# The up-projection of a gated MLP by seven block products in place of eight

## The chip, the cores and the metric

The kernel runs on one core of a Trainium2 chip. The metric is the device time of one execution in microseconds (us). Below, PE is the matrix engine, DVE the vector engine, ACT the scalar engine, POOL the GpSimd engine and SP the engine that only issues DMAs here.

## The reference, cut to what matters

One layer of a hybrid backbone on 128 context tokens and 512 latent tokens: a token mixer (retention beside attention, merged, projected) and then the MLP that the change is about. Both groups of tokens use the same weights and only the modulation differs, so the kernel treats them as 640 columns.

```python
def conv_ffn(h, w_up, conv_w, conv_b, w_down):      # h (L, 1024), w_up (1024, 5632), w_down (2816, 1024)
    L = h.shape[1]
    u = h @ w_up
    up = jnp.pad(u, ((0, 0), (1, 1), (0, 0)))
    uc = conv_w[0] * up[:, :L] + conv_w[1] * up[:, 1:L + 1] + conv_w[2] * up[:, 2:L + 2] + conv_b
    a, g = jnp.split(uc, 2, axis=-1)
    return (jax.nn.silu(g) * a) @ w_down
...
        h = rmsnorm(xs, norm2_g[l]) * (1.0 + sc2) + sh2
        xs = xs + g2 * conv_ffn(h, w_up[l], conv_w[l], conv_b[l], w_down[l])
```

The result then passes a last RMSNorm with `final_g`.

## The kernel before, in words

All matrices are fp32. A product of two fp32 matrices is made of three PE products of rounded parts: each operand is split into a high part (a cast) and a low part (the operand minus its high part), and high·high, high·low and low·high are summed in PSUM. A weight block of 128 x 1024 is loaded as `raw` (2 buffers), cast by ACT into a `wh` tile (L143) and its low part subtracted by DVE into another `wh` tile (L148); there are 8 `wh` tiles. In the variant "dma", ACT writes the negated high part (L145) and a DMA issued from POOL adds `raw` to it (L146).

The region of the change is the second half of the program. First comes the output projection with the second normalisation: `h2_norm` (L1031 to L1034) scales a block of 128 tokens, `h2_trans` (L1043 to L1055) transposes it on PE and writes the high and low parts of the activations, h, as `hT` (128 x 8 x 640 each). Then the MLP: its 2816 channels are 22 blocks f of 128. For each f and each half i (i = 0 the part `a`, i = 1 the gate `g`), `up_cols` makes u = w_up·h by two PSUM tiles of 320 columns of tokens, of 24 matmuls each (8 blocks of the depth times 3, L1107 to L1109); ACT copies them into a `u` tile (L1113, L1114) that has zero columns between and around the two sequences. `up_gate` is the convolution of three taps (ACT L1121, DVE L1122 and L1123), then gating (ACT tanh L1127, DVE L1128 and L1129) and the split of the gated tile `gt` into high (ACT L1130) and low (POOL L1131). For f = 0 and 1 `up_cols` runs first on 256 columns, between the last transposes, and then on 384.

The down-projection takes a group of f (2, then 4 at a time): ten PSUM tiles of 512 columns with 12 matmuls per group of four, each then multiplied by a gate row and added to the residual by DVE (L1168, L1169). Up- and down-projection alternate: the up-projection of the next four f, then the down-projection of the four before. In the last group `square` (L1174) and `finish` (L1178 to L1188) make the last RMSNorm. `gate_rows` (L270) makes the gate rows between the first f and the loop, on PE.

The order of PE's instructions is the order of the code in the stretches under `manual_schedule`; elsewhere a scheduler sets each engine's queue when the program is built. Every engine takes its queue in order. PSUM has eight tiles of 512 columns: before, 3 for the up-projection (`mm`) and 5 for the down-projection (`acc`).

## Time and profile before

| what | value |
|---|---|
| median of three runs | 1215.33 us (1214.75 to 1215.36) |
| the profiled execution's own time | 1216.4 us |
| its span in the trace | 1214.6 us |
| PE busy | 1181.1 us, 97% of the span |
| DVE busy | 679.3 us, 56% |
| ACT busy | 488.0 us, 40% |
| POOL busy | 138.3 us, 11% |

The span is the time from the first to the last instruction that the trace shows; the execution's own time has another 1.8 us around it. A timeline row has a start, a duration, an engine, a line, the operation, what it writes and reads, its shape, and in brackets the idle time of its engine just before it with what ended it. Matmuls overlap, so the time that one takes of PE is read from the distance of two starts and not from its duration.

### The profile page before, as it was taken

Reading aid. Unit: us, or ns where it says so; the run is one execution under the profiler, and the core shown is the slowest. Engines: PE = TensorE matmul, PEld = TensorE weight load, DVE = VectorE, ACT = ScalarE, POOL = GpSimd, SP = SyncE. Lnnn points to the kernel's source line nnn. Section 1 sums busy time; section 2 is a strip of 40 time slices with the busy share of each in tenths; the row PEclk is TensorE's granted clock in tenths of the full one; section 3 lists DMA queues with packets and bytes.
Section 4 is the critical chain, followed back from the end, with each engine's and each line's share of the span. In section 5 each row is a group of like instructions: output and inputs, shape, how many; then the busy total and the mean of one; then the engine's idle time right before and its main releaser. Section 6 shows DMA issues by size and latency. Waiting matters only on the chain.

```text
span 1214.6 us, 18211 instructions
## 1 busy us (share of the span) xinstructions
PE 1181.1 (97%) x7545; PEld 1071.4 (88%) x7545; DVE 679.3 (56%) x1211; ACT 488.0 (40%) x881; POOL 138.3 (11%) x142
## 2 busy tenths in 40 slices
PE   4999999999999999999999999999999999999995
PEld 3788899999988888789999889999989989989984
...
GB/s 284 260 117 70 36 35 36 36 70 206 170 191 140 150 85 73 6 70 68 72 70 70 156 71 158 70 63 111 70 72 67 70 105 55 85 71 97 76 1 87
DMA packets 106387, 115.42 MB, mean 95 GB/s; under 512 B 25136, under 2 KB 77440, under 8 KB 106304
## 3 DMA queue, kind: packets, MB, share of 16 engines
...
## 4 chain that ended last, share of the span: by engine, by line
PE 93%; DVE 3%; ACT 1%; issue 1%; POOL 1%; DMA 0%; SPq 0%; DVEq 0%; ACTq 0%; POOLq 0%
DMA xin.u1.1_112<-in_x_sample 0%; POOL f0.s.5_3525 L898 0%; ACT gt.gt0.2_6393 L1051 0%; DVE x1.u1.1_6381 L1027 0%; PE mm1.mm.11_318 L155 0%; DVE acts.u2.2_101 L1055 0%; PE mm1.mm.11_318 L157 0%; POOL f0.s.5_3525 L921 0%; PE mm3.mm.40_4503 L155 0%; PE mm3.mm.36_4220 L155 0%; PE mm3.mm.22_3753 L155 0%; PE mm3.mm.40_4503 L157 0%; PE mm3.mm.37_4500 L155 0%; PE mm1.mm.12_319 L155 0%; PE mm3.mm.37_4500 L157 0%
## 5 line engine op out<-in xcount | busy, mean ns | idle before, releaser
L787 POOL TENSOR_TENSOR ret.r2k.6_3635<-ret.u5.5_3528,ret.u1.1_3521 128x256 f32<-128x256 f32 x2 | 1.4, 737 | 204.3 <-ACT ret.u5.5_3528 L783 204.3
L1184 POOL TENSOR_TENSOR x1.u1.1_6381<-x1.u1.1_6381,t7.u6.6_6913 128x512 f32<-128x512 f32 x5 | 6.4, 1285 | 43.4 <-ACT x1.tm.95_10737 L1174 23.5
L836 DVE SCALAR_TENSOR_TENSOR ret2.u1.1_4322<-ret2.u1.1_4322,const.u14.14_94 64x128 f32<-64x128 f32 x24 | 6.8, 338 | 6.4 <-ACT ret2.u1.1_4322 L829 6.3
L352 PE MATMUL mm1.mm.1_180<-const.u1.1_70,xin.u1.1_112 128*128 128x128 f32 x4 | 1.1, 435 | 9.3 <-DVE xin.u1.1_112 L345 9.3
L838 DVE SCALAR_TENSOR_TENSOR ret2.u1.1_4322<-ret2.u1.1_4322,const.u14.14_94 64x128 f32<-64x128 f32 x24 | 6.6, 379 | 4.7 <-ACT ret2.u1.1_4322 L831 4.7
L148 DVE TENSOR_TENSOR weights.wh.183_6567<-weights.raw.181_6564,weights.wh.182_6566 128x1024 fp32r<-128x1024 f32 x1 | 1.2, 1226 | 14.2 <-ACT weights.wh.182_6566 L143 14.2
L352 PEld LDWEIGHTS mm1.mm.1_180<-const.u1.1_70,xin.u1.1_112 128*128 128x128 f32 x4 | 0.7, 218 | 9.5 <-DVE xin.u1.1_112 L345 9.5
L389 ACT CAST acts.u1.1_100<-f0.s.1_113 128x640 fp32r<-128x640 f32 x4 | 2.9, 729 | 14.3 <-DVE f0.s.1_113 L387 14.3
L789 DVE TENSOR_TENSOR ret.u5.5_3528<-ret.u5.5_3528,ret.u1.1_3521 128x512 f32<-128x512 f32 x5 | 3.5, 692 | 9.2 <-POOL ret.r2k.8_3706 L787 3.2
L789 DVE TENSOR_TENSOR ret.u4.4_3527<-ret.u4.4_3527,ret.u1.1_3521 128x512 f32<-128x512 f32 x5 | 3.5, 692 | 8.9 <-POOL ret.r2k.11_3886 L787 4.7
L521 POOL TENSOR_TENSOR p1.u1.1_618<-p1.u3.3_622,p1q.u1.1_612 128x512 f32<-128x512 f32 x1 | 1.3, 1297 | 60.8 <-DMA p1.vc.6_627<-in_cache_v 60.8
L898 POOL TENSOR_TENSOR f0.s.5_3525<-f0.s.5_3525,ret2.ny20.11_4904 128x512 f32<-128x512 f32 x5 | 6.0, 1237 | 9.1 <-DVE ret2.ny20.11_4904 L215 9.1
L490 ACT ACTIVATE f0.s.3_724<-f0.s.3_724,p1q.ny20.11_892 128x128 f32<-128x128 f32 x20 | 6.0, 389 | 2.5 <-DVE p1q.ny20.11_892 L213 2.5
L148 DVE TENSOR_TENSOR weights.wh.108_4352<-weights.raw.106_4349,weights.wh.107_4351 128x1024 fp32r<-128x1024 f32 x1 | 1.2, 1226 | 10.1 <-ACT weights.wh.107_4351 L143 10.1
L389 ACT CAST acts.u1.1_100<-f0.s.2_114 128x640 fp32r<-128x640 f32 x4 | 2.9, 728 | 9.8 <-DVE f0.s.2_114 L387 9.8
L1055 DVE TENSOR_TENSOR acts.u2.2_101<-gt.gt0.2_6393,acts.u1.1_100 128x512 fp32r<-128x512 f32 x10 | 6.8, 686 | 0.0
L1131 POOL TENSOR_TENSOR gt.gt1.14_9296<-t7.tg.51_9431,gt.gt0.13_9295 128x641 fp32r<-128x641 f32 x1 | 2.0, 1952 | 39.3 <-PE mm7.mm.58_9464 L1108 39.3
L1131 POOL TENSOR_TENSOR gt.gt1.12_8594<-t7.tg.39_8729,gt.gt0.11_8593 128x641 fp32r<-128x641 f32 x1 | 1.9, 1936 | 39.2 <-PE mm7.mm.42_8762 L1108 39.2
L143 ACT CAST weights.wh.112_4507<-weights.raw.111_4505 128x1024 fp32r<-128x1024 f32 x1 | 1.0, 1047 | 13.0 <-PE mm3.mm.36_4220 L156 13.0
L255 DVE COPY mod2.wr.9_4312<-aux3.aux.15_4279 128x128 f32<-128x128 f32 x1 | 0.3, 292 | 10.7 <-PE aux3.aux.15_4279 L252 10.7
L336 ACT ACTIVATE acts.u2.2_101<-xin.u1.1_112 128x1024 fp32r<-128x1024 f32 x5 | 5.3, 1056 | 2.5 <-DMA xin.u1.1_112<-in_x_prompt 1.7
L490 ACT ACTIVATE f0.s.4_973<-f0.s.4_973,p1q.ny20.20_1141 128x128 f32<-128x128 f32 x20 | 6.2, 399 | 0.0
...
## 6 DMA issues: line engine op xcount, KB each, us to landing
xin.u1.1_112<-in_x_sample SPq DMA_DIRECT2D x4, 512.0 KB
...
```

What stands on the lines that cost most here:

```text
L148: (lo_eng or V).tensor_sub(lo, rv, hi.bitcast(F32))
L336: nc.scalar.activation(sq, xin[:, t, :], AF.Square, accum_out=ss[:, t:t + 1])
L352: nc.tensor.transpose(ps[:, j * P:(j + 1) * P], xin[:, t, k * P:(k + 1) * P], ident)
L389: nc.scalar.copy(hT[0][:, k, :], xk)
L490: nc.scalar.activation(x[:, j], x[:, j], AF.Copy, scale=rstd[:, j:j + 1])
L789: V.tensor_mul(z, z, r1[:, t, 0:1, :].to_broadcast([P, 8, 64]))
L836: V.scalar_tensor_tensor(Ss[0:64, hh, st + 1, j], Ss[0:64, hh, st, j], cdsel[0:64, h:h + 1], Ss[0:64, hh, st + 1, j], op0=ALU.mult, op1=AL ...
L838: V.scalar_tensor_tensor(Ss[64:128, hh, 2 - st, j], Ss[64:128, hh, 3 - st, j], cdsel[64:128, h:h + 1], Ss[64:128, hh, 2 - st, j], op0=ALU. ...
L898: nc.gpsimd.tensor_mul(ov, ov, rso[:, 4 * t:4 * t + 4].unsqueeze(2).to_broadcast([P, 4, P]))
L1055: V.tensor_sub(d[1], h3, d[0].bitcast(F32))
L1131: nc.gpsimd.tensor_sub(gt[1][:, fi, :641], tg, gt[0][:, fi, :641].bitcast(F32))
L1184: nc.gpsimd.tensor_mul(x1[:, t, lo], x1[:, t, lo], fg[:, lo])
```

## The change

The 2816 channels are 11 pairs of f. For 9 of the 11 pairs (f = 4 to 21), and for each half i of these, the product of 256 output channels, a depth of 1024 and the tokens is made by Strassen's method: channels, depth and tokens are each halved, and seven products of sums of blocks replace the eight products of blocks. Such a product of a pair and a half is called a unit below; there are 18.

- To halve the tokens evenly, h is stored with the zero columns that the convolution wants: two halves of 322 columns (`HW`), so `h2` is 128 x 8 x 644 and a PSUM tile has 322 columns.
- Four sums of activation blocks are made once (`diff`, `neg_sum`, `hi_of`, `lo_of`, L1168 to L1184): DVE instructions on 128 x 1288 elements, eleven ahead of the loop and three more later, with their high parts on ACT.
- `unit_group` makes a unit. Its products come in the order 1, 5, 6, 2, 7, 3, 4, each 12 matmuls of 322 columns. The weight blocks are summed in place by four DVE additions (128 x 4 x 128, L1285) per unit. A product's weights are one `wh` tile with a high half (ACT L1288) and a low half: by DVE (L1293) for five products, and for products 2 and 3 by ACT (L1290) and an accumulating DMA from POOL (L1291).
- Products share PSUM tiles: 1, 6, 7 and 4 accumulate one after another in one tile, 5 and 3 in a second, 2 has a third. Between them partial sums are copied out: ACT copies after 1 (L1312), 6 (negated, L1316), 7 (L1320) and 4 (L1324) and after 5 (negated, L1314), and DVE adds or subtracts after 2 (L1318), 7 (L1321) and 3 (L1330). Product 6 therefore starts only when ACT has copied the tile after 1, 7 when it has copied after 6, and 4 when it has copied after 7. One other product lies between each two of them on PE.
- PSUM is four `mm` and four `acc` tiles. The `wh` tiles are filled ahead of their use as the 8 buffers allow (`pump`): eight products ahead in the units.
- The down-projection's weights are split with "dma" in all groups but the last. The gated tiles hold two f in place of four; gating writes into the tiles of the convolution.
- In the last group f = 18 and 19 come first for the first four token blocks, in eight PSUM tiles, then f = 20 and 21 are added to each. The columns of the projection ahead of the MLP are made one token block earlier (`out_half`), and the low parts of the first weights are placed elsewhere there.

```diff
+        def prod(m):
+            def go():
+                q = {1: 1, 6: 1, 7: 1, 4: 1, 2: 2, 5: 3, 3: 3}[m]
+                if m in (1, 2, 5):
+                    st[q] = mm([P, 512], tag="mm")[:, :HW]
+                ps, (ah, al), (bh, bl) = st[q], AOP[m], ops[m]
+                for k in range(4):
+                    nc.tensor.matmul(ps, bh[:, k], ah[:, k], start=m in (1, 2, 5) and k == 0, stop=False,
+                                     skip_group_check=m in (3, 4, 6, 7))
...
+                if m == 1:
+                    nc.scalar.copy(u[0][:, lo_u], ps)
+                elif m == 5:
+                    nc.scalar.activation(u[1][:, hi_u], ps, AF.Copy, scale=-1.0)
+                elif m == 6:
+                    nc.scalar.activation(u[1][:, lo_u], ps, AF.Copy, scale=-1.0)
+                elif m == 2:
+                    V.tensor_add(u[0][:, lo_u], u[0][:, lo_u], ps)
+                elif m == 7:
+                    nc.scalar.copy(u3[i], ps)
+                    V.tensor_sub(u[1][:, hi_u], u[1][:, hi_u], u3[i])
+                    V.memset(u[1][:, 642:643], 0)
+                elif m == 4:
+                    nc.scalar.copy(u[0][:, hi_u], ps)
...
+                else:
+                    V.tensor_sub(u[1][:, lo_u], u[1][:, lo_u], ps)
...
+                if add:
+                    V.tensor_add(src, src, bs[add])
+                t_ = wp([P, 1024], F32R, tag="wh", bufs=8)
+                hi, lo = (t_[:, z * 512:(z + 1) * 512].rearrange("p (k n) -> p k n", n=P) for z in range(2))
+                nc.scalar.copy(hi, src)
+                if m in (2, 3):
+                    nc.scalar.activation(lo, src, AF.Copy, scale=-1.0)
+                    nc.gpsimd.dma_start(lo, src, accum_op=ALU.add)
+                else:
+                    V.tensor_sub(lo, src, hi.bitcast(F32))
...
+    groups = [plain_group(1, 0)] + down_groups([0, 1]) + [plain_group(1, 1)]
+    for p in range(2, NF // 2):
+        groups.append(unit_group(p, 0))
+        if p % 2:
+            groups += down_groups(list(range(2 * p - 4, 2 * p)))
+        groups.append(unit_group(p, 1))
...
+        for t in range(NT - 1):
+            for c0, n in cols[t]:
+                last_mm(t, c0, n, (0, 1))
+        for t in range(NT):
+            for c0, n in cols[t]:
+                last_mm(t, c0, n, (2, 3) if t < NT - 1 else (0, 1, 2, 3))
+                down_add(bank[t, c0], t, c0)
```

ACT's queue in the middle of the loop, before: two f of the up-projection. `weights.wh` are the weight tiles, `mm7` the PSUM tiles, `cv` the convolution's tiles, `tg` the tanh, `gt` the gated tiles.

```order
L1127 ACTIVATE t7.tg.39_8729<-t7.cv.38_8725 128x641
L1113 COPY t7.u3.3_6898<-mm7.mm.41_8735 128x128
L1114 COPY t7.u3.3_6898<-mm7.mm.41_8735 128x192
L143 CAST weights.wh.264_8857<-weights.raw.263_8855 128x1024
L1130 CAST gt.gt0.11_8593<-t7.tg.39_8729 128x641
L143 CAST weights.wh.266_8861<-weights.raw.263_8855 128x1024
L1114 COPY t7.u3.3_6898<-mm7.mm.42_8762 128x320
```

The same queue in the changed kernel, one unit (its tile for products 1, 6, 7 and 4 is mm.37, that for 5 and 3 mm.38, that for 2 mm.39):

```order
L1312 COPY t7.u1.1_6919<-mm7.mm.37_9190 128x322
L1314 ACTIVATE t7.u3.3_6921<-mm7.mm.38_9212 128x322
L1288 CAST weights.wh.310_9205<-weights.raw.300_9046 128x512
L1141 CAST gt.gt0.17_9155<-t7.cv.36_8825 128x641
L1316 ACTIVATE t7.u3.3_6921<-mm7.mm.37_9190 128x322
L1138 ACTIVATE t7.tg.41_9230<-t7.cv.40_9208 128x641
L1288 CAST weights.wh.311_9227<-weights.raw.300_9046 128x512
L1288 CAST weights.wh.312_9249<-weights.raw.300_9046 128x512
L1290 ACTIVATE weights.wh.312_9249<-weights.raw.300_9046 128x512
L1288 CAST weights.wh.313_9268<-weights.raw.300_9046 128x512
L1320 COPY const.u1.1_70<-mm7.mm.37_9190 128x322
```

A PSUM tile's copy had two or three instructions on weights and gating ahead of it in the queue; each of the copies L1316 and L1320 now has between one and five ahead of it since the copy before, and a product of PE waits for each.

DVE's queue in the middle of the loop, before:

```order
L1128 SCALAR_TENSOR_TENSOR t7.tg.51_9431<-t7.tg.51_9431,t7.cv.50_9427 128x641
L1129 TENSOR_TENSOR t7.tg.51_9431<-t7.tg.51_9431,t7.cv.49_9423 128x641
L148 TENSOR_TENSOR weights.wh.295_9560<-weights.raw.293_9557,weights.wh.294_9559 128x1024
L148 TENSOR_TENSOR weights.wh.297_9564<-weights.raw.293_9557,weights.wh.296_9563 128x1024
L1122 SCALAR_TENSOR_TENSOR t7.cv.52_9543<-t7.u3.3_6898,t7.u5.5_6912,t7.cv.52_9543 128x641
```

And in the changed kernel, beside the ACT rows above (same unit):

```order
L1129 SCALAR_TENSOR_TENSOR t7.cv.40_9208<-t7.u2.2_6920,t7.u5.5_6927,t7.cv.40_9208 128x641
L1139 SCALAR_TENSOR_TENSOR t7.cv.38_9163<-t7.tg.39_9184,t7.cv.38_9163 128x641
L1285 TENSOR_TENSOR weights.raw.300_9046<-weights.raw.300_9046 128x4x128
L1140 TENSOR_TENSOR t7.cv.36_8825<-t7.cv.36_8825,t7.cv.38_9163 128x641
L1293 TENSOR_TENSOR weights.wh.310_9205<-weights.raw.300_9046,weights.wh.310_9205 128x512
L1130 SCALAR_TENSOR_TENSOR t7.cv.40_9208<-t7.u2.2_6920,t7.u5.5_6927,t7.cv.40_9208 128x641
L1285 TENSOR_TENSOR weights.raw.300_9046<-weights.raw.300_9046 128x4x128 x2
L1139 SCALAR_TENSOR_TENSOR t7.cv.40_9208<-t7.tg.41_9230,t7.cv.40_9208 128x641
L1293 TENSOR_TENSOR weights.wh.311_9227<-weights.raw.300_9046,weights.wh.311_9227 128x512
L1140 TENSOR_TENSOR t7.cv.37_8855<-t7.cv.37_8855,t7.cv.40_9208 128x641
L1318 TENSOR_TENSOR t7.u1.1_6919<-t7.u1.1_6919,mm7.mm.39_9253 128x322
```

ACT's casts L1288 now wait for DVE's sums L1285, and its cast L1141 for DVE's product L1140; on DVE these stand between the convolutions and the low parts.

DVE's queue at the start of the loop, in the changed kernel. The 1288 elements are sums of activation blocks; `weights.wh.204` is the low part of the second half of the weights of the first plain group, f = 2 and 3:

```order
L1170 TENSOR_TENSOR gt.gt0.5_7252<-gt.gt0.5_7252,acts.u2.2_101 128x1288
L1130 SCALAR_TENSOR_TENSOR t7.cv.8_7212<-t7.u3.3_6921,t7.u5.5_6927,t7.cv.8_7212 128x641
L1129 SCALAR_TENSOR_TENSOR t7.cv.9_7216<-t7.u4.4_6922,t7.u5.5_6927,t7.cv.9_7216 128x641
L1184 TENSOR_TENSOR sums.u4.4_6913<-gt.gt1.6_7253,sums.u3.3_6912 128x1288
L1130 SCALAR_TENSOR_TENSOR t7.cv.9_7216<-t7.u4.4_6922,t7.u5.5_6927,t7.cv.9_7216 128x641
L1184 TENSOR_TENSOR sums.u6.6_6915<-gt.gt0.5_7252,sums.u5.5_6914 128x1288
L1139 SCALAR_TENSOR_TENSOR t7.cv.7_7208<-t7.tg.10_7270,t7.cv.7_7208 128x641
L151 TENSOR_TENSOR weights.wh.204_7293<-weights.raw.199_7284,weights.wh.203_7292 128x1024
```

Before, only the convolutions and the gating of f = 0 and 1 stood there; the low part of those weights now comes behind the eleven sums.

## Rows read from the trace of the kernel before

**Rows 1.** The page's busy time of the engines, with the share of the span and the count of instructions, and the engines' shares of the chain that ended last.

```profile
PE 1181.1 (97%) x7545; PEld 1071.4 (88%) x7545; DVE 679.3 (56%) x1211; ACT 488.0 (40%) x881; POOL 138.3 (11%) x142
...
PE 93%; DVE 3%; ACT 1%; issue 1%; POOL 1%; DMA 0%; SPq 0%; DVEq 0%; ACTq 0%; POOLq 0%
```

**Rows 2.** PE's waits: what waited for what, the sum in us, the count, the longest. The longest of all, and the only one behind 650 us.

```profile
PE mm1.mm.1_180 L352 <- DVE xin.u1.1_112 L345: 9.3, 1, 9.3
...
PE aux3.aux.99_7036 L1043 <- DVE gt.gt0.1_6392 L1034: 1.1, 1, 1.1
```

**Rows 3.** Busy time by stretch: the stretch and its length, busy time of PE, PEld, DVE, ACT and POOL with counts, the granted clock of PE, the DMA share, GB/s. The loop, and the out-projection ahead of the MLP.

```profile
766.00:1180.00 414.00, 414.00 (x2492) 388.57 (x2491) 251.36 (x286) 163.26 (x266) 36.01 (x23) 1.00 0.23 74
...
700.00:746.00 46.00, 44.87 (x264) 39.41 (x263) 36.82 (x115) 22.65 (x51) 7.50 (x18) 1.00 0.62 94
```

**Rows 4.** PE's timeline in the loop: the first matmuls of two tiles of the up-projection that follow each other, of 24 matmuls each.

```profile
850.52 0.31 PE L1107 MATMUL mm7.mm.25_8033<-acts.u1.1_100,weights.wh.224_7895 128*128 128x320 f32 x1
...
854.04 0.31 PE L1107 MATMUL mm7.mm.26_8060<-acts.u1.1_100,weights.wh.224_7895 128*128 128x320 f32 x1
```

**Rows 5.** ACT's timeline in the loop: a PSUM copy, the first tap of a convolution, tanh, the cast of a gated tile, the cast of a weight block.

```profile
850.72 0.43 ACT L1114 COPY t7.u2.2_6897<-mm7.mm.24_7993 128x320 f32<-128x320 f32 x1 [3.03 <-PE mm7.mm.24_7993 L1109]
851.18 0.93 ACT L1121 ACTIVATE t7.cv.26_8023<-t7.u2.2_6897,t7.u5.5_6912 128x641 f32<-128x641 f32 x1
854.05 0.74 ACT L1127 ACTIVATE t7.tg.27_8027<-t7.cv.26_8023 128x641 f32<-128x641 f32 x1 [1.94 <-DVE t7.cv.26_8023 L1123]
...
856.81 0.73 ACT L1130 CAST gt.gt0.9_7891<-t7.tg.27_8027 128x641 fp32r<-128x641 f32 x1
857.61 1.05 ACT L143 CAST weights.wh.236_8159<-weights.raw.233_8153 128x1024 fp32r<-128x1024 f32 x1
```

**Rows 6.** DVE's timeline in the loop: a tap, a step of the gating, two low parts of weights; and POOL's low part of a gated tile, which ran beside the second of them.

```profile
852.14 0.89 DVE L1122 SCALAR_TENSOR_TENSOR t7.cv.26_8023<-t7.u2.2_6897,t7.u5.5_6912,t7.cv.26_8023 128x641 f32<-128x641 f32 x1 [5.23 <-ACT t7.cv.26_8023 L1121]
...
854.82 0.83 DVE L1128 SCALAR_TENSOR_TENSOR t7.tg.27_8027<-t7.tg.27_8027,t7.cv.26_8023 128x641 f32<-128x641 f32 x1 [0.87 <-ACT t7.tg.27_8027 L1127]
...
856.93 1.23 DVE L148 TENSOR_TENSOR weights.wh.235_8156<-weights.raw.233_8153,weights.wh.234_8155 128x1024 fp32r<-128x1024 f32 x1 [0.42 <-ACT weights.wh.234_8155 L143]
858.70 2.00 DVE L148 TENSOR_TENSOR weights.wh.237_8160<-weights.raw.233_8153,weights.wh.236_8159 128x1024 fp32r<-128x1024 f32 x1 [0.54 <-ACT weights.wh.236_8159 L143]
...
857.66 1.96 POOL L1131 TENSOR_TENSOR gt.gt1.10_7892<-t7.tg.27_8027,gt.gt0.9_7891 128x641 fp32r<-128x641 f32 x1 [24.56 <-PE mm7.mm.26_8060 L1108]
```

**Rows 7.** The timelines of four engines ahead of the loop: PE's last matmul on tile mm.96; ACT's instructions up to its copy of that tile and one copy of 512 columns; a tap on DVE that lay beside POOL's low part of a gated tile.

```profile
762.38 0.34 PE L1109 MATMUL mm3.mm.96_7163<-acts.u1.1_100,weights.wh.196_6927 128*128 128x384 f32 x1
...
761.89 1.05 ACT L145 ACTIVATE weights.wh.204_7270<-weights.raw.202_7267 128x1024 fp32r<-128x1024 f32 x1
762.85 1.03 ACT L143 CAST weights.wh.205_7274<-weights.raw.202_7267 128x1024 fp32r<-128x1024 f32 x1
763.79 0.47 ACT L1114 COPY t7.u4.4_6899<-mm3.mm.96_7163 128x384 f32<-128x384 f32 x1
764.16 0.58 ACT L272 COPY gate.u1.1_5311<-mm7.mm.1_7228 128x512 f32<-128x512 f32 x1
...
761.18 2.23 DVE L1123 SCALAR_TENSOR_TENSOR t7.cv.10_7206<-t7.u3.3_6898,t7.u5.5_6912,t7.cv.10_7206 128x641 f32<-128x641 f32 x1
...
761.13 1.59 POOL L1131 TENSOR_TENSOR gt.gt1.6_7191<-t7.tg.9_7200,gt.gt0.5_7190 128x641 fp32r<-128x641 f32 x1 [21.47 <-ACT gt.gt0.5_7190 L1130]
```

**Rows 8.** The last group's timelines: PE's first matmuls of two tiles of the down-projection, of 12 matmuls each and 512 columns; DVE's evacuation of a tile; the first `finish` on DVE, its end and what comes behind it; the last evacuation, of 256 columns.

```profile
1181.75 0.39 PE L155 MATMUL acc7.acc.54_10775<-weights.wh.349_10711,gt.gt0.15_9997 128*128 128x512 f32 x1
...
1184.54 0.39 PE L155 MATMUL acc7.acc.55_10793<-weights.wh.344_10701,gt.gt0.15_9997 128*128 128x512 f32 x1
...
1187.60 0.69 DVE L1168 TENSOR_TENSOR x1.tm.102_10806<-acc7.acc.55_10793,gate.u1.1_5311 128x512 f32<-128x512 f32 x1 [1.38 <-PE acc7.acc.55_10793 L157]
1188.33 0.69 DVE L1169 TENSOR_TENSOR x1.u1.1_6381<-x1.u1.1_6381,x1.tm.102_10806 128x512 f32<-128x512 f32 x1
...
1194.52 0.16 DVE L1178 TENSOR_REDUCE t7.ss3.73_10847<-x1.u3.3_6383 128x3 f32<-128x9 f32 x1
...
1200.20 0.68 DVE L1168 TENSOR_TENSOR x1.tm.108_10894<-acc7.acc.58_10881,gate.u1.1_5311 128x512 f32<-128x512 f32 x1
...
1203.79 0.43 DVE L1168 TENSOR_TENSOR x1.tm.114_10948<-acc7.acc.61_10935,gate.u1.1_5311 128x256 f32<-128x256 f32 x1
```

**Rows 9.** Timelines at the start of the MLP: the last scaling of a token block on DVE; PE's first matmul on 384 columns, and its first of the gate rows behind 96 such; DVE's last low part of the activations.

```profile
741.14 0.75 DVE L1034 TENSOR_SCALAR gt.gt0.1_6392<-x1.u1.1_6381,x1.ny1.42_6877 128x1024 f32<-128x1024 f32 x1
...
745.75 0.34 PE L1107 MATMUL mm3.mm.93_7085<-acts.u1.1_100,gt.gt1.3_6586 128*128 128x384 f32 x1
...
762.56 0.61 PE L270 MATMUL mm7.mm.1_7228<-const.u1.1_70,const.u6.6_86 128*128 128x128 f32 x4
...
745.96 0.69 DVE L1055 TENSOR_TENSOR acts.u2.2_101<-gt.gt0.2_6393,acts.u1.1_100 128x512 fp32r<-128x512 f32 x1
```

**Rows 10.** The chain of waits: one of the four stretches of gate rows on PE (start, length, tile, line).

```profile
762.72 0.89 PE mm7.mm.1_7228 L270 x8
```

**Rows 11.** DMA issues: an accumulating DMA from POOL, its size and the us from issue to landing.

```profile
weights.wh.204_7270<-weights.raw.202_7267 POOLq DMA_DIRECT2D x1, 512.0 KB, 4.5
```

334 lines of the change are left out of this document (224 added, 110 removed).

## The prediction, made before the changed kernel ran

> **What bounds the kernel now.** I read the page's busy shares first, then PE's waits, then busy time by stretch, and last the timelines of the loop, since the change lies there. PE is busy for 97% of the span and is 93% of the chain that ended last [rows 1]; its longest wait behind the first microseconds is 1.1 us, ahead of the MLP [rows 2]. In the loop from 766 to 1180 us PE is busy for 414.00 of 414 us at a granted clock of 1.00, while DVE is busy for 251 (61%) and ACT for 163 (39%) [rows 3]. So every microsecond of matmul taken from the loop comes off the time, as long as DVE and ACT deliver weights and copies in time. The reader is to see that PE never waits in the loop, that DVE has some 160 us of idle time there, and that each tile of the up-projection costs the other engines one copy only.
>
> **Matmuls removed.** Two tiles' starts lie 854.04 − 850.52 = 3.52 us apart for 24 matmuls of 320 columns, 0.1467 us each [rows 4]. A tile of the down-projection takes 2.79 us for 12 of 512, 0.2325 each [rows 8]: per column 0.458 and 0.454 ns, so columns set the price, and 322 cost 0.1476. A unit had 4 tiles of 24, 14.08 us, and has 84 matmuls, 12.40 us. That is 1.68 us less, and for 18 units **−30.2 us**. The two pairs that stay get 4 more columns in each of 8 x 24 matmuls: 192 x 4 x 0.458 ns = **+0.35**.
>
> **Handovers in a unit.** This is the wait that the change adds. A product lasts 12 x 0.1476 = 1.77 us. Product 6 may start when ACT has copied the shared tile after 1, and product 5 lies between; so ACT has 1.77 us from one product's end to the next one's start. A copy of 320 columns takes 0.43 us and begins 0.2 us after the next tile's first matmul (850.72 against 850.52 [rows 4, 5]): ACT may come 1.1 us late at no cost. What stands ahead of the copy in ACT's queue decides. Casts of half a tile: 0.58 us by the copy of 512 columns [rows 7]; a tap 0.93, tanh 0.74, the cast of a gated tile 0.73 [rows 5]. Rows 7 show such a lateness: the copy of mm.96 began at 763.79, though its last matmul had started at 762.38 and lasted 0.34, because two weight instructions of 1 us stood ahead. One instruction of that kind fits into the slack and two do not.
>
> Worse is an instruction ahead of the copy that itself waits for DVE: ACT's cast of a block sum waits for DVE's addition, and the cast of the gated tile for DVE's product. DVE's load in four units: 36 additions and low parts of 512 at 0.69 [rows 8] = 24.8; 12 evacuations of 322 columns, between 0.43 for 256 and 0.69 for 512 [rows 8], 0.50 = 6.0; 16 taps at 0.89 and 8 gating steps at 0.83 [rows 6] = 20.9. That is 51.7 us in 49.6 us of PE. Queued independent instructions start a little closer than their durations (1188.33 − 1187.60 = 0.73 is a dependent pair), so 48 to 52. Behind four units come two groups of the down-projection, 10 tiles x 2.79 = 27.9 us, with 20 x 0.69 = 13.8 us of DVE: over the period of 77.5 us DVE has 65.5, 85%. ACT has in four units 36 x 0.58 + 20 x 0.43 + 8 x 0.93 + 4 x 1.47 = 42.8 us, 86%. Weights are made eight products, 14 us, ahead, so PE will not starve for weights; the copies, in the same queues, have no such lead.
>
> I followed both queues by hand through a period in the order in which they stand, with these durations, each instruction starting when its engine was free and its inputs were there. With the durations whole, the four units lost 0.3, 0.4, 1.2 and 1.7 us = 3.6; with successive instructions overlapping by a tenth, 0, 0, 0.95 and 0.95 = 1.9. The late ones are those in which gating and the sums of the next unit meet. For 4.5 periods: 8.6 to 16 us. The bounds lie further apart: nothing, if the queues interleave better than I followed, and 38 (rival C). I take **+14**, near the upper figure, since DVE is at 97% to 105% of PE's time in the units.
>
> **The start.** DVE is busy for 36.8 of 46 us in the out-projection [rows 3], and the scaling that releases the last transposes at 741.14 [rows 9] ended PE's 1.1 us [rows 2]. Two low parts of 1.23 us [rows 6] now stand in that stretch: +2.4 (0 to 4). Then the first plain group wants its second weights 17.0 us (4 tiles of 388 columns, from 16.81 for 384 [rows 9]) + 3.6 (four stretches of 0.89 [rows 10]) + 1.8 = 22.4 us after the 388-column tiles begin. On DVE their low part stands behind eleven sums of 1288 elements, 1.5 us each (1.23 for 1024 [rows 6], scaled), eight taps, one gating step and itself: 16.5 + 7.1 + 0.8 + 1.2 = 25.7, from 0.9 us on when the last h is written [rows 9]. So 2.3 to 4.2 us late; I take 3.3, and 0.3 for the first unit. Together **+6** (2 to 10).
>
> **The end.** Before, DVE waits 1.38 us for each tile of 2.79 us and needs 2 x 0.69 for it [rows 8]. Now the second passes have 6 matmuls, 1.40 us a tile, against DVE's 1.38 plus 0.04 between: DVE has no reserve, meets `finish`, a run of 5.7 us on DVE (1194.52 to 1200.20 [rows 8]), later against PE, and ends later behind PE's last matmul. At most it lags by two tiles: 0 to 3, taken **+1.5**. The gating of f = 20 and 21 is covered by eight first passes, 11.2 us.
>
> **What costs nothing.** The accumulating DMAs land 4.5 us after their issue [rows 11]; their cover is the lead of 14 us, and without it each would cost what it exceeds. The loads from memory have the same bytes at 74 GB/s [rows 3]; `final_g` moves to the end. The gated tiles in pairs come free with the down-projection that stands ahead of their next use.
>
> **The sum.** −30.2 + 0.35 + 14 + 6 + 1.5 = −8.3. The profiled execution took 1216.4 us, its span 1214.6 and 1.8 around it; so 1208.1 for one like it. The median of the runs lies 1.1 below the profiled execution: **1207 us**.
>
> **Rivals.** *B, nearly all is kept*: the queues drift so that the copies find ACT free. For it: the lead of 14 us lets weight work wait, and over a period DVE is at 85% and ACT below that. Against it: queues are in order, and the order is fixed. Then the term of 14 falls to 0 and 1193 us comes out.
>
> *C, slower*: ACT waits for DVE ahead of the copies. Its place is each of the three handovers of a unit; its price two taps of DVE at 0.89 ahead of the sum for which ACT's cast waits, less the slack of 1.1: 0.7 us a handover, 2.1 a unit, 38 in all. That gives 1215.3 − 30.2 + 0.35 + 38 + 7.5 = 1231. It decides from (30.2 − 0.35 − 7.5) / 18 = 1.24 us a unit. For it: DVE's full load in the units. Against it: by the queues only two of four units lose more than 0.5.
>
> *D, no change*, by DVE and POOL in each other's way. DVE's low part took 2.00 beside POOL's in place of 1.23 [rows 6], 0.77 more; a tap took 2.23 in place of 0.89 [rows 6, 7], 1.34 more. The units have 18 gated tiles. The smaller figure I count among what the 14 and its bounds hold; the larger would add (1.34 − 0.77) x 18 = 10 us of DVE, which, all passed to PE, gives 1217. For it: the full load of DVE. Against it: in the loop the rows show the smaller figure. The Trainium skill's "SBUF — State Buffer", section "SBUF: two separate sides", says that a GpSimd instruction and a DVE one with two SBUF operands lock the shared ports for a whole instruction and the other blocks fully. By that rule the tap's row is the normal case and D follows; the trace agrees for the tap (2.23 us), and for the low part only halfway, since POOL's own instruction was also longer there (1.96 against 1.59 us).
>
> **Chances and range.** A, the forecast (1200 to 1212.9): 0.46; B 0.19; D 0.13; C 0.22. A difference of 0.2% (2.4 us) is about what can be told from none. Faster is A and B, 0.65; the same is D, 0.13; slower C, 0.22. The range runs from 1190, below B by the start's lower bound, to 1227, where C costs 1.9 us a unit; a tenth is left out on either side.
>
> **What would show it.** PE's busy time lower by about 30 us, and its idle time in the loop near 14 us, at the first matmuls of products 6, 7 and 4, put down to ACT's lines 1312, 1316 and 1320, most of it in the two units ahead of a down-projection: then the handovers are right. Waits on DVE's L1293 or L1285 in the loop would say that weights are late and the lead is used up. One wait of 2 to 4 us on `weights.wh.204` shows the start. DVE's share in the units should be above 90%. The prediction is wrong if PE shows no idle time in the units (B), if it loses over 1.2 us in each (C), or if the pitch of 322 columns is not 0.148 us.

## The result: 0.4% slower

The changed kernel takes 1220.21 us (median of 6 runs, 1219.09 to 1221.7), the kernel before 1215.34 beside it: ratio 1.0041, 95% interval [1.0028, 1.0054]. The profiled execution took 1221.7 us, its span is 1219.9. The forecast of 1207 was wrong in sign; the time lies within the range.

The page after, busy time and chain, beside [rows 1]:

```profile
PE 1165.2 (96%) x7329; PEld 1046.6 (86%) x7329; DVE 773.4 (63%) x1450; ACT 553.9 (45%) x999; POOL 201.5 (17%) x184
...
PE 74%; DVE 13%; ACT 4%; issue 4%; DMA 3%; POOL 1%; SPq 0%; DVEq 0%; ACTq 0%; POOLq 0%
```

PE does 216 matmuls less, but it was 93% of the chain and is 74%: DVE, ACT and DMAs now stand on the path. PE's busy time by stretch, beside [rows 3], and its waits, beside [rows 2]:

```profile
766.00:1180.00 414.00, 399.83 (x2331) 368.59 (x2330) 334.81 (x511) 234.67 (x394) 98.16 (x74) 1.00 0.56 123
700.00:746.00 46.00, 39.79 (x199) 33.57 (x198) 35.02 (x101) 19.62 (x41) 6.26 (x9) 0.94 0.41 70
```

```profile
PE aux3.aux.97_6973 L1047 <- DVE gt.gt1.2_6393 L1038: 4.8, 1, 4.8
PE mm7.mm.5_7312 L1120 <- DVE weights.wh.204_7293 L151: 2.4, 1, 2.4
...
PE mm7.mm.52_10087 L1307 <- ACT t7.u2.2_6920 L1312: 1.1, 1, 1.1
PE mm7.mm.55_10223 L1307 <- ACT const.u1.1_70 L1320: 1.1, 1, 1.1
```

PE never waited in the loop; now it is idle for 14.17 us of it, 2.4 for the weights of the first plain group, the rest ahead of products. The 4.8 us at aux.97 stand in the out-projection. The time between landmarks of the two traces gives the terms of the sum:

| term | forecast | measured | read from |
|---|---|---|---|
| matmuls of 18 units, wider plain pairs | −29.85 | −29.85 (taken as forecast) | a product without a wait lasts 1.76 to 1.79 us, a unit of them 12.43, as against 12.40 |
| handovers | +14 | +18.74 | the units take 241.94 us; 18 x 12.40 = 223.2 |
| start | +6 | +11.7 | gate rows at 772.55, were at 762.56 [rows 9], less the row below: 7.45; the first four plain tiles take 18.58, the next four 14.33: 4.25 |
| 512-column matmuls before 673 us | none | +2.55 | the same tiles begin that much later |
| end | +1.5 | +2.14 | 15.28 us behind PE's last matmul, were 13.14 |
| sum, of the span | −8.3 | +5.3 | 1219.9 − 1214.6 |

Where the last rows of the handovers come from shows in the timelines around one late product, PE's mm.52 (product 6), which ACT's L1312 releases:

```profile
1079.95 1.76 POOL L1142 TENSOR_TENSOR gt.gt1.22_9908<-t7.cv.49_9607,gt.gt0.21_9907 128x641 fp32r<-128x641 f32 x1 [0.46 <-ACT gt.gt0.21_9907 L1141]
...
1079.78 0.48 DVE L1321 TENSOR_TENSOR t7.u3.3_6921<-t7.u3.3_6921,const.u1.1_70 128x322 f32<-128x322 f32 x1
...
1080.59 1.66 DVE L1285 TENSOR_TENSOR weights.raw.342_9798<-weights.raw.342_9798 128x512 f32<-128x512 f32 x1
...
1082.28 0.62 ACT L1288 CAST weights.wh.357_10057<-weights.raw.342_9798 128x512 fp32r<-128x512 f32 x1 [1.02 <-DVE t7.u1.1_6919 L1325]
1082.81 0.93 ACT L1128 ACTIVATE t7.cv.54_10062<-t7.u3.3_6921,t7.u5.5_6927 128x641 f32<-128x641 f32 x1
1083.63 0.61 ACT L1288 CAST weights.wh.359_10080<-weights.raw.350_9913 128x512 fp32r<-128x512 f32 x1
1084.15 0.92 ACT L1128 ACTIVATE t7.cv.55_10083<-t7.u1.1_6919,t7.u5.5_6927 128x641 f32<-128x641 f32 x1
1084.97 0.41 ACT L1312 COPY t7.u2.2_6920<-mm7.mm.52_10087 128x322 f32<-128x322 f32 x1
...
1085.43 0.41 PE L1307 MATMUL mm7.mm.52_10087<-sums.u3.3_6912,weights.wh.353_9979 128*128 128x322 f32 x1 [1.08 <-ACT t7.u2.2_6920 L1312]
```

Read it from above: while POOL makes the low part of a gated tile, DVE's block sum takes 1.66 us (0.68 elsewhere); ACT's cast of that sum stands 1.02 us waiting (its bracket names L1325, a small memset that DVE made as the sum ended), three more instructions of ACT follow it, and the copy on which PE waits comes last. From the first gate row to the end of the last unit, DVE's instructions that last longer than the median of their line exceed it by 20.1 us in all, 12.4 of it at L1285; this is called DVE's excess below. It is counted in this way for every run; the recorded expectations have 20.8, 16.9 and 9.7 where this count gives 20.1, 21.3 and 9.6.

The start's wait is in the chain of waits:

```profile
728.67 1.14 DVE weights.wh.193_6804 L1092
729.84 7.30 DMA weights.raw.199_7284<-in_w_up
737.22 1.06 ACT weights.wh.201_7288 L146
738.30 1.23 DVE weights.wh.202_7289 L151
...
742.56 0.67 DVE gt.gt1.2_6393 L1038
743.28 1.11 PE aux3.aux.97_6973 L1047 x4
```

The low part that the change moved to a later block (L1092) keeps a load buffer until 729.8. Only then the next load starts; ACT's cast and DVE's low part wait for it at the head of their queues, and the normalising of the last token block but one (L1038), for which PE waits, queues behind them.

### The profile page after: what moved, and what is told of

It is laid out like the page before. It is cut to its first block, busy times and chain, and to the rows that moved or that the text cites. A ratio compares the mean times of both kernels' runs of the same rounds, so it can differ in the third digit from the quotient of the medians.

```text
span 1219.9 us, 18328 instructions
## 1 busy us (share of the span) xinstructions
PE 1165.2 (96%) x7329; PEld 1046.6 (86%) x7329; DVE 773.4 (63%) x1450; ACT 553.9 (45%) x999; POOL 201.5 (17%) x184
## 4 chain that ended last, share of the span: by engine, by line
PE 74%; DVE 13%; ACT 4%; issue 4%; DMA 3%; POOL 1%; SPq 0%; DVEq 0%; ACTq 0%; POOLq 0%
DVE x1.u1.1_6381 L1218 1%; DMA weights.raw.199_7284<-in_w_up 1%; DMA weights.wh.244_8024<-weights.raw.232_7804 1%; DMA weights.raw.366_10197<-in_w_down 0%; DMA weights.raw.324_9445<-in_w_down 0%; DMA weights.raw.282_8693<-in_w_down 0%; DMA xin.u1.1_112<-in_x_sample 0%; DMA weights.raw.404_10963<-in_w_down 0%; POOL f0.s.5_3525 L901 0%; DVE weights.raw.216_7428 L1285 0%; DVE gt.gt0.5_7252 L1170 0%; DVE gt.gt0.5_7252 L1168 0%; DVE x1.u1.1_6381 L1236 0%; ACT const.u1.1_70 L1320 0%; PE mm1.mm.11_318 L158 0%
## 5 line engine op out<-in xcount | busy, mean ns | idle before, releaser
L1321 DVE TENSOR_TENSOR t7.u3.3_6921<-t7.u3.3_6921,const.u1.1_70 128x322 f32<-128x322 f32 x9 | 8.1, 895 | 10.0 <-ACT const.u1.1_70 L1320 10.0
L1233 POOL TENSOR_TENSOR x1.u1.1_6381<-x1.u1.1_6381,weights.raw.409_10973 128x512 f32<-128x512 f32 x5 | 7.5, 1493 | 15.2 <-ACT x1.tm.122_11171 L1223 7.1
L493 ACT ACTIVATE f0.s.3_724<-f0.s.3_724,p1q.ny20.11_892 128x128 f32<-128x128 f32 x20 | 6.0, 388 | 2.5 <-DVE p1q.ny20.11_892 L216 2.5
```

The source lines that it names most:

```text
L493: nc.scalar.activation(x[:, j], x[:, j], AF.Copy, scale=rstd[:, j:j + 1])
L1233: nc.gpsimd.tensor_mul(x1[:, t, lo], x1[:, t, lo], fg[:, lo])
L1321: V.tensor_sub(u[1][:, hi_u], u[1][:, hi_u], u3[i])
```

## The experiments

All times are medians beside runs of the kernel before; "gate" is when the gate rows begin, "loss" what the 18 units take over 223.2 us; both, and the excess, are those of the one traced execution of each run.

| run | time, us | ratio, 95% | gate | loss | DVE's excess |
|---|---|---|---|---|---|
| before | 1215.3 | | 762.6 | | 9.6 |
| changed | 1220.2 | 1.0041 [1.0028, 1.0054] | 772.6 | 18.7 | 20.1 |
| after_start | 1215.7 | 1.0012 [1.0001, 1.0024] | 769.9 | 19.8 | 21.2 |
| after_layout | 1211.4 | 0.9976 [0.9961, 0.9991] | 766.3 | 18.3 | 21.3 |
| after_no_pool | 1210.5 | 0.9953 [0.9938, 0.9968] | 774.8 | 7.7 | 0.7 |
| after_no_sums | 1207.3 | 0.9934 [0.9918, 0.9950] | 774.6 | 4.2 | 12.7 |
| after_low_on_dve | 1207.5 | 0.9935 [0.9919, 0.9951] | 766.8 | 15.2 | 0.7 |
| after_early_sums | 1216.1 | 1.0019 [1.0005, 1.0033] | 766.8 | 22.5 | 21.6 |
| after_early_low_dve | 1201.6 | 0.9887 [0.9873, 0.9902] | 767.0 | 9.8 | 0.7 |
| after_early_low_dma | 1216.7 | 1.0017 [1.0006, 1.0027] | 764.8 | 11.7 | 0.7 |
| after_handovers_only | 1214.6 | 0.9998 [0.9986, 1.0009] | 772.5 | 9.3 | 0.7 |

**The slower matmuls far ahead of the change.** The tiles of activations moved and grew from 20480 to 20608 bytes of a partition. First matmuls of the same two tiles, three tiles of 12 apart, before and after:

```profile
334.19 0.39 PE L155 MATMUL mm3.mm.18_3533<-weights.wh.72_3539,acts.u1.1_100 128*128 128x512 f32 x1
...
342.35 0.39 PE L155 MATMUL mm3.mm.21_3536<-weights.wh.72_3539,acts.u1.1_100 128*128 128x512 f32 x1
```

```profile
334.35 0.39 PE L158 MATMUL mm3.mm.18_3533<-weights.wh.72_3539,acts.u1.1_100 128*128 128x512 f32 x1
...
342.67 0.39 PE L158 MATMUL mm3.mm.21_3536<-weights.wh.72_3539,acts.u1.1_100 128*128 128x512 f32 x1
```

8.16 us became 8.32. Shifting the tiles by widening the constants' tile that lies ahead of them (786 for 782 columns in the kernel before, 794 for 786 in the changed one) tests the place alone; lengthening the tiles of the kernel before tests the length.

```diff
-    hT = [hp([P, KD, TOK], F32R) for _ in range(2)]
+    hT = [hp([P, KD * 644], F32R)[:, :KD * TOK].rearrange("p (k t) -> p k t", k=KD) for _ in range(2)]
```

before_shifted: 

> The kernel before with one edit: the constants' tile is four columns wider (786 in place of 782), as in the changed kernel, so that every tile behind it lies 32 bytes further on. Theory 1: the addresses cost the 2.5 us that the changed kernel has lost by its output projection; a tile of the input projection takes 2.77 us in place of 2.72, and the time is 1215.3 + 2.5 = about 1217.8. Rival: the tiles' 2.77 us come from something else of the changed kernel (its larger activation tiles) or from the run; then 2.72 stays, and 1215.3.

after_shifted: 

> The changed kernel with the constants' tile eight columns wider still (794), which puts the weight tiles back to the same place modulo 64 bytes as before. Theory 1: the tiles of the input projection take 2.72 us again and 2.5 us come back, 1220.2 - 2.5 = 1217.7. Rival: 2.77 stays, and 1220.2.

before_padded: 

> The kernel before with one edit: each of the two activation tiles has 644 in place of 640 columns for each of the 8 blocks, the rest as it was. The tiles of the input projection take 2.77 us in the changed kernel and 2.72 before; a shift of all tiles by 32 bytes did not do it. Theory 2 (the distance of the two activation tiles, 20608 in place of 20480 bytes, makes the matmuls slower): 2.77 here too, and about 1215.1 + 2.5 = 1217.6. Rival (it is the run or the chip): 2.72, and 1215.

The shifts left the pitch as it was: 1218.39 us (1.0028 [1.0016, 1.0039]; of these 3.3 us over the kernel before, 2.1 arise at the gate rows, where PE now waits 1.5 us) and 1221.32 (1.0054 [1.0039, 1.0069]). With the padding the kernel before has the slow pitch, 2.77 us a tile in place of 2.72:

```profile
334.37 0.39 PE L155 MATMUL mm3.mm.18_3533<-weights.wh.72_3539,acts.u1.1_100 128*128 128x512 f32 x1
...
342.69 0.39 PE L155 MATMUL mm3.mm.21_3536<-weights.wh.72_3539,acts.u1.1_100 128*128 128x512 f32 x1
```

It is 2.47 us late by 553 us, and takes 1221.48 us (1.0053 [1.0038, 1.0068]), more than the 1217.6 expected: trace against trace it is 4.8 us longer, 2.2 of it at the gate rows, where PE waits 1.6 us. So the tile's length does it, in either kernel. Whether by itself or by where it puts the tiles behind it isn't separated (shifts by four and eight columns alone were tried), and why is open.

**The start.** after_dma_split makes the plain groups' low parts by accumulating DMA; after_start also makes their casts depend, through two small POOL instructions, on the h of the last block but one, so that they can't stand ahead of it in the queues; after_layout, on top of after_start, pads the activation tiles to 22528 bytes.

```diff
-            st["w"] = w_split(st["raw"], 8, 256)
+            if i == 0:
+                z, x = t7([P, 2]), h2[1][:, 7, 508:510].bitcast(F32)
+                nc.gpsimd.tensor_sub(z, x, x)
+                nc.gpsimd.tensor_add(st["raw"][:, ::1024], st["raw"][:, ::1024], z)
+            st["w"] = w_split(st["raw"], 8, 256, "dma")
...
-    hflat = [hp([P, KD * 2 * HW], F32R) for _ in range(2)]
+    hflat = [hp([P, 5632], F32R)[:, :KD * 2 * HW] for _ in range(2)]
```

after_dma_split: 

> The changed kernel; the weights of the two plain groups (f = 2 and 3) have their low parts made by ACT and POOL's accumulating DMA, so DVE has no weight instruction in its queue ahead of the loop that waits for their load. Theory 1: the wait of 4.8 us on the last scaling of a token block, most of that of 1.4, the wait of 2.4 on the second half of the weights and the half clock behind both (about 4 us) go: 8 to 11 us less, 1209 to 1212. Rival (DVE's sums and low parts are simply too many at the start): the waits move to other DVE instructions and under 3 us come back, 1217 or more.

after_start: 

> The changed kernel with the low parts of the plain groups' weights by the accumulating DMA (as in after_dma_split) and one thing more: two instructions on POOL, of no effect on the values, let the casts of the first plain group's weights depend on activations that the last but one transposed block writes, so that in ACT's queue they stand behind that block. Theory 2 (at the start it is not DVE's load: the load of those weights comes 7 us later than its casts were planned for, and what stands in the queue behind the cast waits with it): the wait of 4.8 us (3.7 in after_dma_split) ahead of the transposes falls under 1.5, with it the half clock, and the gate rows begin at 766 or earlier in place of 772.3; 1220.2 - 4.4 (wait on the second half of the weights and its clock) - 6 = about 1210. Rival (DVE has too much to do in that stretch): the wait stays above 3 us, and the gate rows begin at 771 or later; 1216 or more.

after_layout: 

> The kernel of run after_start (1215.7 us), with its two activation tiles padded from 5152 to 5632 columns of 4 bytes (22528 bytes of a partition). The 512-column matmuls of the in-projection took 2.72 us a tile of 12 before the change, and 2.77 with the widened tiles, in the kernel before too. Theory 'the length of the activation tile sets where it and what lies behind it stand in the memory, and some such places cost the reads 1.5%': with another length the tiles may go back to 2.72, the gate rows come 2.4 us earlier, and the time is 1213. Rival 'it is the distance of the block rows in the tile (322 columns in place of 320) or the width itself': the tiles stay at 2.77 and the time at 1215 to 1216.

after_dma_split (1219.42, 1.0030 [1.0014, 1.0045]) has no wait on wh.204, but 3.7 us at aux.97: the cast still stands in ACT's queue, waiting for its load. Its first down-projection begins at 790.2 in place of 794.6, but in the traced execution the units lose 23.1 us, with one wait of 4.7 on L1320, so its time says little of the start. after_start cuts the wait at aux.97 to 2.5 us and begins the first down-projection at 787.8: 4.5 us gained, between its theory and its rival, so the load is shown as a part of the late start and not as the whole. In after_layout the tiles are back at 8.16 us for three (333.55 to 341.71), and 4.3 us are gained, more than the 2.4 expected: the units lost 1.5 less as well, and no half clock followed the wait at aux.97, as 3.4 us of it did in after_start.

**Handovers by more room.** after_apart gives each product a PSUM tile of its own (sums of products are left out, so that no product waits for a copy); after_apart_dve adds low parts of the down weights by DVE; after_act_order fixes ACT's order as the code stands, with gating in two pieces; after_interleaved, on top of after_layout, interleaves two units.

```diff
-                if m in (1, 2, 5):
-                    st[q] = mm([P, 512], tag="mm")[:, :HW]
+                st[q] = mm([P, 512], tag="mm")[:, :HW]
...
```

after_apart: 

> The changed kernel; each of the seven products has a PSUM tile of its own, four tiles in turn, so no product waits for a copy of the tile that it adds to (left out: that the products in one tile are summed). Copies and all other work stay. Theory 1 (handovers): the 18.7 us by which the 18 units are longer than 18 x 12.40 fall to under 4, 1220.2 - 15 = 1205. Rival (DVE at its limit): the waits move to weights or to free PSUM tiles, over 10 of the 18.7 stay, 1212 or more.

after_apart_dve: 

> As after_apart (each product its own PSUM tile; left out: that products are summed), and the low parts of the down-projection's weights by DVE in place of ACT and the accumulating DMA. After_apart had units of 12.44 us, but 13 us of waits on those DMAs at the first tiles of four down-projections. Theory 2 (behind the handovers these DMAs are what is late next): the first tiles of the down-projections take under 3.5 us, and the time falls by 9 to 12 from after_apart's profiled 1216, to about 1205. Rival (DVE at its limit): with 2.46 us more of DVE per group the waits turn up on DVE's low parts of weights, and the time stays within 4 us of after_apart.

after_act_order: 

> The changed kernel with ACT's order in the loop as the code stands (copies first, then the casts of the next weights; the gating in two pieces), in place of the scheduler's. Nothing is left out. Theory 1 (the order of ACT's queue makes the handovers late): their 18.7 us fall to 10 or less; but as the down-projection's weights are late next, no more than 3 to 6 us of the time come back: 1214 to 1217. Rival (what ACT waits for, DVE's sums, decides): 18.7 stays or grows, 1220 or more.

after_interleaved: 

> The kernel of run after_layout, with the two units of a pair interleaved, so that between a product and the one that needs its copied tile at least two others stand (A1 A2 B1 A5 B5 A6 B6 A3 A7 B7 B3 A4 B2 B4), the tiles of products in five banks and the down-projection's in three, the down-projections after every second pair, and the low parts of half of the down weights on DVE. All of the reference is computed. Theory 'the handovers are late by one or two ACT instructions, about 1 to 2 us each, and room of one more product hides them': the pair takes 2 x 12.4 to 2 x 12.6 us, no wait on L1312, L1316 or L1320 above 0.3 us, and the time is 1200 to 1208 us, below both kernels, unless the weights come late. Rival 'ACT and DVE are short of time over the whole period': the loss moves to the weights of the down-projection or to the last copies, the loop is as long as in after_layout, and the time is 1211 or more.

after_apart: units of 12.44 us, loss 0.7, so the shared tiles are the whole of the handover term. Yet it takes 1218.92 us (1.0034 [1.0021, 1.0047]; the traced execution 1215.98): the first tiles of the down-projections take 5.4 to 6.8 us for 2.79, waiting for accumulating DMAs, 12.9 us given back. One of these waits:

```profile
PE acc7.acc.31_9655 L159 <- DMA weights.wh.326_9564<-weights.raw.316_9343: 2.2, 1, 2.2
```

With these low parts on DVE the first tiles wait for POOL's gated low parts instead (9.3 us given back; 1213.03, 0.9985 [0.9975, 0.9994]). Weights and gating are hardly ahead: they take what PE gains. after_act_order takes 1260.56 us (1.0374 [1.0356, 1.0392]), with a loss of 55.6; the order that I wrote down was worse than the scheduler's. after_interleaved takes 1220.17 (1.0041 [1.0026, 1.0056]): four waits of 2.6 to 3.9 us on DVE's L1327 in place of most of those on ACT, as the rival had it. In that kernel, against what its expectation says, one convolution in four read the upper half of its tile before product 7 was added.

**What makes the copies late.** after_no_pool puts zeros for POOL's low part of a gated tile, after_no_sums leaves the weight sums out.

```diff
-        nc.gpsimd.tensor_sub(r[1], ca, r[0].bitcast(F32))
+        nc.gpsimd.memset(r[1].bitcast(F32), 0)
```

after_no_pool: 

> The changed kernel, in which POOL's low part of a gated tile (L1142) is a memset of zeros that reads nothing; the low part itself is left out. In the changed kernel DVE's instructions of the loop last 20.8 us longer in all than the medians of their kinds, most of them beside this line. Theory 'POOL stretches DVE, and through the sums that ACT's casts wait for it makes the copies late': the excess falls to near 0, the loss of the 18 units (18.7 us over 18 x 12.40) to 10 or less, and the time to about 1212 us. Rival 'the queues' order alone makes the loss': the excess falls, the loss stays above 15 us, and the time within 3 us of 1220. A memset writes too, so part of the excess may stay; a result between the two shares the loss.

after_no_sums: 

> The changed kernel without the additions and subtractions of weight blocks on DVE (L1285): the sums of the weights are left out, each cast takes the block as loaded. Theory 'the copies come late because ACT's cast ahead of them waits for DVE's sum': the waits of PE on L1312 and L1320 nearly vanish, the loss of the units falls below 6 us, and the time to 1207 to 1212 us (the start keeps most of its 11.7 us; its sums go too, so some of it may come back). Rival 'the casts that stand ahead of the copies wait for the loads of weights and for the accumulating DMAs, not for the sums': the waits stay, the loss stays above 12 us, and the time is 1215 or more.

Both go as their theories had it: without POOL's reads the excess falls from 20.1 to 0.7 us and the loss from 18.7 to 7.7; without the sums the loss falls to 4.2. The four sums of the unit around mm.49 (shortest, median and longest in ns), changed and after_no_pool:

```profile
L1285 DVE TENSOR_TENSOR weights.raw.342_9798<-weights.raw.342_9798 x4: 679/1170/2059, 1071.3 to 1080.6; 128x512 f32<-128x512 f32 x4
...
L1285 DVE TENSOR_TENSOR weights.raw.342_9798<-weights.raw.342_9798 x4: 683/684/689, 1065.7 to 1073.6; 128x512 f32<-128x512 f32 x4
```

In after_no_sums 12.7 us of excess are left at other lines, with a smaller loss, which fits that a delay costs time only where a cast ahead of a copy waits for it. That run also takes 72 instructions of 0.68 us from DVE, so it doesn't tell the sums' place from their amount. The start is no earlier in either (gate at 774.8 and 774.6).

**A cure that computes everything.** On top of after_layout: the low part of a gated tile on DVE in place of POOL; and each weight sum issued behind the low part of the product before, in place of right ahead of its own cast.

```diff
-        nc.gpsimd.tensor_sub(r[1], ca, r[0].bitcast(F32))
+        V.tensor_sub(r[1], ca, r[0].bitcast(F32))
...
-                if add:
-                    V.tensor_add(src, src, bs[add])
...
                 ops[m] = (hi, lo)
+                n = order[order.index(m) + 1:][:1]
+                if n and PLAN[n[0]][1]:
+                    at, add = PLAN[n[0]]
+                    V.tensor_add(bs[at], bs[at], bs[add])
```

after_low_on_dve: 

> The kernel of run after_layout with the low part of a gated tile by DVE (0.82 us each, as its product L1140) in place of POOL (L1142). Theory 'POOL's instruction is harmful by lengthening DVE's': DVE gets 18 x 0.82 = 14.8 us more work in the units and loses an excess of 16.9, so its sum is about the same; if only the sum counts, the time stays within 2 us of 1211.4. If what counts is the single long delay (an instruction of 2.1 to 2.4 us ahead of a cast), the loss falls from 18.3 to 10 to 13 us and the time to 1204 to 1207.

after_early_sums: 

> The kernel of run after_layout (1211.4 us, units lose 18.3), with each block sum of the weights issued on DVE right behind the low part of the product before, in place of right ahead of its own cast on ACT: same instructions, other order. Theory 'the cast that stands ahead of a copy waits for the sum just ahead of it': the sum is there a product (1.8 us) earlier, so a lengthening of 1 us no longer reaches the copy; the loss falls to 5 to 9 us and the time to 1198 to 1202. Rival 'DVE is late in total, by its lengthened instructions, and where the sum stands doesn't matter': the loss stays above 14 us and the time is 1207 or more.

after_early_low_dve: 

> Both edits of after_early_sums and after_low_on_dve. If the two causes are one chain (POOL lengthens DVE, the sum is late, the cast waits, the copy is late), the second edit adds little to the first: within 3 us of after_early_sums. If they are separate, the gains add up, loss below 5 us, time below 1198.

after_early_low_dma: 

> The edit of after_early_sums, and the low part of a gated tile by ACT (a negated rounded copy, 0.73 us as the cast L1141) and an accumulating DMA in place of POOL's subtraction. DVE loses POOL's excess and gets no work; ACT gets 18 x 0.73 = 13.1 us. Theory 'DVE is the engine whose lateness counts': loss below 5 us, time 1196 to 1199, if the DMA (4.5 to 7.4 us) is there before the down-projection. Rival 'ACT's queue is as full, and each instruction more ahead of a copy costs': loss above 9 us or first tiles of the down-projection above 4 us, time above 1202.

Neither theory foresaw after_early_sums: the sums alone, moved earlier, cost 4.6 us. Its timelines ahead of one of four waits of 3.0 us:

```profile
984.27 2.92 POOL L1142 TENSOR_TENSOR gt.gt1.18_9164<-t7.cv.37_8832,gt.gt0.17_9163 128x641 fp32r<-128x641 f32 x1 [7.60 <-ACT gt.gt0.17_9163 L1141]
987.16 1.98 POOL L1142 TENSOR_TENSOR gt.gt1.18_9164<-t7.cv.38_8862,gt.gt0.17_9163 128x641 fp32r<-128x641 f32 x1
...
984.34 0.68 DVE L1300 TENSOR_TENSOR weights.raw.300_9053<-weights.raw.300_9053 128x512 f32<-128x512 f32 x1
984.94 0.82 DVE L1140 TENSOR_TENSOR t7.cv.38_8862<-t7.cv.38_8862,t7.cv.41_9216 128x641 f32<-128x641 f32 x1
985.72 2.03 DVE L1295 TENSOR_TENSOR weights.wh.311_9234<-weights.raw.300_9053,weights.wh.311_9234 128x512 fp32r<-128x512 f32 x1
987.67 2.02 DVE L1300 TENSOR_TENSOR weights.raw.300_9053<-weights.raw.300_9053 128x512 f32<-128x512 f32 x1
...
989.76 0.62 ACT L1290 CAST weights.wh.313_9275<-weights.raw.300_9053 128x512 fp32r<-128x512 f32 x1 [2.40 <-issue]
990.28 0.42 ACT L1326 COPY const.u1.1_70<-mm7.mm.37_9198 128x322 f32<-128x322 f32 x1
```

The new order brings POOL's two low parts together beside two instructions of DVE (2.03 and 2.02 us) that stand ahead of one cast, the second of them its sum, and the copy L1326 behind that cast is late by both. Take POOL away and the same order gains: after_early_low_dve, 1201.6 us, is 6.0 below after_low_on_dve (1207.5), 1.1% below the kernel before and 18.7 us below the changed one. It is 14.5 us below after_early_sums, so the second edit isn't a small addition to the first; but with a loss of 9.8, where under 5 was expected, the gains don't simply add up either. Five waits are left in its units, four of them of 1.2 us; two of these:

```profile
PE mm7.mm.25_8446 L1313 <- ACT const.u1.1_70 L1326: 1.2, 1, 1.2
PE mm7.mm.37_9198 L1313 <- ACT const.u1.1_70 L1326: 1.2, 1, 1.2
```

after_low_on_dve itself gains 3.9 us, less than its theory's 4.4 to 7.4, and its loss of 15.2 is above that theory's 10 to 13. after_no_pool, which spares DVE the 14.8 us as well, lost 7.7 from a later start. This suggests that DVE's amount of work counts too, and not only its single long delays; no run separates it from the other changes in the queues. after_early_low_dma goes as its rival had it, with a loss of 11.7, and brings waits elsewhere: four first tiles of the down-projections take 4.0 to 5.3 us, waiting for the gated tiles' DMA. The traced execution, at 1213.1 us, is the shortest of ten; what the others have on top, 3.7 us in the median, is in no trace.

Two controls:

after_handovers_only: 

> The changed kernel with the two edits of after_early_low_dve alone (early sums, low part of a gated tile on DVE), and neither the edits of the start nor the padded tiles. If the terms are independent, the loss of the units falls from 18.7 to 9.8 us as there, the late start and the slower 512-column matmuls stay, and the time is 1220.2 - 8.9 = 1211.3 (1209 to 1213). If the start or the layout are worth nothing by themselves, it is 1201 to 1204; if the handovers gain only with a good start, 1216 or more.

before_low_on_dve: 

> The kernel before with the low part of a gated tile on DVE in place of POOL. Its trace has an excess of DVE's instructions beside POOL too (9.7 us), with DVE at 61% in the loop and PE never waiting. Theory 'the lengthening costs time only by the copies for which a product waits': no effect, 1214 to 1216.5. Rival 'it costs time in any case, by late weights or evacuations': 1 to 5 us faster.

after_handovers_only is the changed kernel with the two handover edits alone. The loss falls by 9.4 us as expected, the time by 5.6, to 1214.6 where 1209 to 1213 were expected: the terms aren't quite independent, since in the first down-projection PE now waits 1.3 and 1.1 us for DVE's evacuation (L1217), which it did not in the changed kernel. before_low_on_dve takes 1215.32 us (1.0005 [0.9995, 1.0015]): in the kernel before, with an excess of 9.6 us, taking POOL's instruction away is worth nothing; in both traces no matmul waits in the loop.

## Why the prediction was wrong

**Right.** The pitch of 322 columns (0.148 us), the price of a product, and so the 30 us that matmuls are worth. Where the handovers fail: L1312 and L1320, though never L1316, and most in the units ahead of a down-projection (units 8 to 11 lose 0, 0.8, 1.8 and 1.8 us). DVE's load over a period (65.6 us measured, 65.5 worked out), by luck: 4.3 us of the measured load are excess, which the sum did not have. The wait on `weights.wh.204` (2.4 us, forecast 3.3). C's price falls: a unit loses 1.04 us on average, not 2.1; but slower, which the prediction gave to C alone, is what came out.

**"Handovers in a unit" was mis-sized, +14 for 18.7.** The replay by hand gave 8.6 to 16 with undisturbed durations, and after_no_pool, whose durations are undisturbed, loses 7.7. What it lacked is POOL: 18.7 − 7.7 = 11.0 us. That is rival D's mechanism, which the prediction set against the forecast, as if the one excluded the other. They add: 14 was said to hold "the smaller figure" of POOL's price, but the replay never followed POOL's queue. D's larger figure makes 1.34 x 18 = 24 us of DVE, all passed to PE; measured are 20.1 us of excess, of which 11.0 come through. That 1220 lies near D's 1217 is in part luck: of the 13.6 us by which the sum was off, 4.7 are the handovers, 5.7 the start, 2.55 the earlier matmuls and 0.6 the end.

The Trainium skill's "SBUF — State Buffer", section "SBUF: two separate sides", has this as a rule: of a GpSimd instruction that reads SBUF and a DVE one with two SBUF inputs, whichever starts first has the shared ports for its whole length, and the other blocks. The trace agrees more closely than the prediction took it to. DVE's sum (two SBUF operands) began 0.64 us into POOL's 1.76 and ended 0.54 us behind it; L1318 and L1330, of the same size as L1321 but with a PSUM operand, have excesses below 0.1 us in 18 each, L1321 3.7. POOL's own instruction stretches by the same rule, from 1.57 to 1.76 us where DVE's L1321 had begun 0.17 us ahead of it, and to 2.92 in after_early_sums, beside two DVE instructions that keep their lengths of 0.68 and 0.82; the first of these is recorded 0.07 us behind POOL's start, so which of the two had the ports can't be read from the starts alone. [rows 6] show this too: POOL began at 857.66, when the first of the two low parts still ran, until 858.16. The prediction took POOL's 1.96 us there as agreeing only halfway.

DVE's share in the units was 83% (44.9 of 54.0 us), not above 90%.

**"The start" was out of its bounds, 2 to 10, at 11.7, and is the largest single miss.** I priced the two moved low parts as 2.4 us of DVE. What counted was the buffer that one of them releases: a load 23 us later than the one before it, which takes 7.3 us beside other loads, and two in-order queues stopped behind it. Then two waits were followed by half the clock, which no term had. The granted clock around the first:

```profile
740.00:741.00 1.00, 0.00 (x0) 0.00 (x0) 0.90 (x7) 0.72 (x3) 0.00 (x0) 0.88 1.09 201
...
742.00:743.00 1.00, 0.00 (x0) 0.00 (x0) 1.00 (x4) 0.40 (x2) 0.00 (x0) 0.50 1.14 8
...
746.00:747.00 1.00, 1.00 (x7) 1.00 (x7) 1.00 (x6) 0.00 (x0) 0.00 (x0) 0.50 0.86 6
...
748.00:749.00 1.00, 1.00 (x10) 1.00 (x10) 1.00 (x5) 0.00 (x0) 0.00 (x0) 1.00 0.86 6
```

PE is idle from 738.5 to 743.3 us, the clock goes to the lower level (0.50, 1.2 GHz), and seven matmuls run in a microsecond where ten did, until 747.6. The wait of 2.4 us at 778.4 is followed by the same from 782 to 785: the four plain tiles lost 4.25 us, of which 2.4 is the wait.

**"What costs nothing" missed two things.** The size of the activation tiles (2.55 us) was taken for a detail of the convolution's zeros. And the accumulating DMAs took up to 8.8 us in the loop, for the 4.5 of [rows 11]: PE hardly waits for them in the changed kernel, where it is late anyway, but it does in after_apart.

**PE's busy time** fell by 15.9 us, not 30. The slow pitch, the half clock and first products behind a wait, which last 1.86 to 1.90 us in place of 1.77, are counted as busy. Idle time alone understates such waits: 11.7 of the 18.7 us that the units lose are idle.
